# The down projection of a hybrid decoder block: eight products of halves, or seven with weight sums made in DRAM

## The chip, the cores and the metric

The kernel runs on one core of one Trainium2 chip. The metric is device time in microseconds (us) of one execution, the median of three runs. A profile comes from one further execution, taken by the hardware profiler; its own time stands in the table below.

## The reference

One decoder layer on 512 tokens of 1024 channels, all in float32. Only the second half matters here:

```python
h = rms_norm(x, g_ffn_pre)
up = h @ w_up                                   # 1024 -> 2 x 3072
gate_h = causal_dwconv(up[..., :D_FF], ffn_conv_w, ffn_conv_b)
hid = jax.nn.gelu(gate_h) * up[..., D_FF:]      # 512 x 3072
x = x + rms_norm(hid @ w_down, g_ffn_post)      # the down projection, 3072 -> 1024
ple_gate = jax.nn.sigmoid(rms_norm(x, g_ple_gate) @ w_ple_gate)
ple = rms_norm(p @ w_ple_proj, g_ple_post)
x = x + ple_gate * ple
```

Before it stand an input projection with a pooling mixer and a gated linear recurrence, their output projections and `w_o`; they are the same in both kernels.

## The kernel before

Every float32 product is made of three matmuls of a narrower type: an operand is split into a high part (`hi`, a cast on ScalarE) and a rest (`lo`, a subtraction on VectorE), and `mm3` issues high x high, high x low and low x high. So each weight block that arrives (`raw`, 128 x 1024) costs ScalarE one cast and VectorE one subtraction before TensorE can use it.

The instructions of TensorE stand in the order of the code. Those of the other engines are put in order by a scheduler that goes by priority, and each engine then runs its own queue strictly in order: an instruction that waits holds up all that stand behind it. `urgent()` raises a priority. Loads are issued from SP's queue; POOL (GpSimd) does nothing but the small power operation of `rsqrt`, twenty times on one column after once on four.

Weights follow one list, `order`, filled by `plan(key, ap)`. `weight(key, ahead)` prepares up to four blocks past the one that is used. `raw`, `hi` and `lo` have six buffers each, so a block's cast can run once TensorE is done with the block six places earlier.

The up projection (`up_product`) already uses seven products in place of eight for each pair of hidden blocks: tokens and channels are halved, sums of weight blocks are formed on VectorE (`add`), and products named 1 to 7 are accumulated and copied between banks. `gated_half` makes the gate (two shifted multiply-adds on VectorE, a gelu on ScalarE) and `hidden` multiplies it into `hid[j]`, for j from 0 to 23.

The down projection before is `token_major("wd", 12, hid_split)`. 24 weight blocks of 256 x 512 are each used by two k-blocks, four token tiles of 128 and `mm3`: 24 x 2 x 4 x 3 = 576 matmuls of 512 columns. Eight banks hold the eight outputs (token tile `t`, half `h`). The last three block pairs run token tile by token tile, so the tiles finish one after another; after each, `add_norm` adds the normed result to the residual `x3`, `x3n` is scaled for the gate, and `x3_tile(t)` transposes it (two times four PE transposes, L710) and splits it for the last product with `w_ple_gate` ("wpg"). Tiles 2 and 3 are transposed after the first two tiles of that last product.

In the names of the rows below, `A` and `C` are large buffers (four of each), `m` are small ones, `ps` are PSUM banks, `t` are temporaries, and `wsum` are the four new tensors in DRAM.

Of the kernel before, what the change touches and what calls it, by code (L numbers as in the profile page):

```python
# [8 lines left out]
F32 = mybir.dt.float32  # L9
# [4 lines left out]
P = 128  # L14
# [21 lines left out]
PLE_AT = 3  # L36

# [30 lines left out]
def block_kernel(  # L68
# [26 lines left out]
    mid = ctx.enter_context(tc.tile_pool(name="mid", bufs=26))  # L95
    tmp = ctx.enter_context(tc.tile_pool(name="tmp", bufs=5))
    small = ctx.enter_context(tc.tile_pool(name="small", bufs=16))
    psum = ctx.enter_context(tc.tile_pool(name="psum", bufs=8, space=bass.MemoryType.PSUM))
# [102 lines left out]

    def seven(p):

        return [(p - (f == 3), f) for f in (SEVEN if p > 1 else SEVEN_1) if (f == 3 or p < NPAIR) and (f != 3 or p > 1)]
# [31 lines left out]
    for kp in range(12):  # L236
        for h in range(2):
            plan(("wd", kp, h), rows2(w_down, kp, h))
# [88 lines left out]


    def rsqrt(v, n=1):
        y = tiny(n)  # L330
        nc.gpsimd.tensor_tensor(y, v, mhalf[:, :n], ALU.pow)  # L331
        return y
# [50 lines left out]
    rstd1 = rsqrt(v4, NT)  # L383
    diag = temp()
# [454 lines left out]
    def hidden(j, pu, q):  # L839
        hid[j] = slot()  # L840
        if q is not None:
            V.tensor_tensor(
                hid[j].rearrange("p (b c) -> p b c", b=2),
                pu.rearrange("p (b c) -> p b c", b=2),
                q[:, None, :].to_broadcast([P, 2, HALF]),
                ALU.add,
            )
            pu = hid[j]
        V.tensor_tensor(hid[j], act_g[j], pu, ALU.mult)
# [33 lines left out]
    for i in range(2):  # L883
        hidden(i, ub[i], None)
# [5 lines left out]

    for p in range(1, NPAIR + 1):
# [11 lines left out]
    g_fpost = gains(G_FFN_POST)  # L903
    ple = [quad("C", F32), quad("C", F32)]
    for a in range(2):
        nc.sync.dma_start(
            ple[a].rearrange("p (a h) c -> p a (h c)", a=2),
            pled[2 * a * P : 2 * (a + 1) * P, :].rearrange("(a p) c -> p a c", p=P),
        )


    x3 = []
    for a in range(2):
        xt = quad("C", F32)
        nc.sync.dma_start(
            xt.rearrange("p (a h) c -> p a (h c)", a=2),
            x2d[2 * a * P : 2 * (a + 1) * P, :].rearrange("(a p) c -> p a c", p=P),
        )
        x3.append(xt)
    g_pg = gains(G_PLE_GATE)  # L920
    hs = {}

    def hid_split(k, t):
        g = k // 4
        if g not in hs:
            hs[g] = quad("A"), quad("A")
            for q in range(4):
                split(hs[g][0][:, q, :], hs[g][1][:, q, :], hid[4 * g + q])
        return tuple(s[:, k % 4, t * P : (t + 1) * P] for s in hs[g])
# [3 lines left out]

    def x3_tile(t):
        for h in range(2):
            ps = transposed(x3n[t, h])
            x3t[t, h] = slot(F32R), slot(F32R)
            with urgent():
                split(*x3t[t, h], ps)

    for t, i, pair in token_major("wd", 12, hid_split):
        if i == 3 and t >= 2:
            x3_tile(t - 2)
        if i != 5:
            continue
        res = [x3[t // 2][:, 2 * (t % 2) + h, :] for h in range(2)]
        with urgent():
            add_norm(pair, g_fpost, res)
            for h in range(2):
                n = slot()  # L950
                V.tensor_tensor(n, res[h], g_pg[h], ALU.mult)
                x3n[t, h] = n
        s3 = rstd_of(res)
        r3[t] = const.tile([P, 1], F32, tag=f"r3{t}", name=f"r3{t}")
        V.tensor_copy(r3[t], s3)
# [97 lines left out]
```

## Time and profile before

| | us |
|---|---|
| median of three runs (lowest, highest) | 765.53 (765.23, 765.67) |
| the profiled execution, its own time | 765.22 |
| its span from first to last instruction | 763.4 |
| TensorE busy in the span | 758.2 (99%) |
| VectorE, ScalarE, POOL busy | 524.0, 406.3, 15.2 |
| mean share of the DMA engines on the one busy queue | 35.9% |
| first matmul of the down projection | 581.21 |
| first matmul of the product with `w_ple_gate` | 713.58 |

Matmuls overlap each other in the records (one of 512 columns is shown as 0.39 us long), so their cost is read from start to start, not from the durations. Stretches of time are given as from:to in us of the span.

### The profile page before, as it was taken

The page shows a single profiled execution, that of the slowest core. Times are in us where ns is not written, and L with a number is a line of the kernel's source. Part 1 is how long each engine was busy: PE and PEld are TensorE (multiplying, and loading weights), DVE is VectorE, ACT ScalarE, POOL GpSimd, SP SyncE. Part 2 cuts the span into 40 slices and gives each one's busy share as a digit, 9 for nine tenths or more (in the row PEclk, how much of TensorE's full clock was granted, in tenths as well). Part 3 has the DMA queues.
Part 4 walks back from the last instruction along what each step waited for, and adds up shares of the span by engine and source line. Part 5 has one row for each costly group of instructions (what it writes and reads, how often), then busy time and mean ns, then how long its engine had stood idle before and what let it go on. Part 6 is the DMA issues. An engine that isn't in the chain of part 4 may idle for free.

```text
span 763.4 us, 11051 instructions
## 1 busy us (share of the span) xinstructions
PE 758.2 (99%) x4377; PEld 669.6 (88%) x4377; DVE 524.0 (69%) x709; ACT 406.3 (53%) x642; POOL 15.2 (2%) x27
## 2 busy tenths in 40 slices
PE   9999999999999999999999999999999999999997
PEld 8887788888888888899999999999999888888886
DVE  4897537998345573589998888888988332335852
ACT  6746779835233251377766666666675322224631
POOL 0000000000000000010000000000000000001100
PEclk9999999999999999999999999999999999999999
DMA  8842222133223449222243233333369332320111
GB/s 333 308 164 82 84 70 84 35 137 124 91 97 124 165 142 327 83 93 80 79 150 104 95 95 111 111 112 111 111 222 316 125 103 91 108 86 0 56 56 55
DMA packets 42163, 93.87 MB, mean 123 GB/s; under 512 B 3456, under 2 KB 4096, under 8 KB 42112
## 3 DMA queue, kind: packets, MB, share of 16 engines
q1 hardware_dynamic: 41968, 93.08, 35.9%
q8 instruction: 34, 0.56, 0.3%
q14 instruction: 17, 0.14, 0.1%
q10 hardware_dynamic: 144, 0.10, 0.0%
HBM read 86.87 MB, written 6.29 MB: 122 GB/s over the span
## 4 chain that ended last, share of the span: by engine, by line
PE 96%; DMA 2%; DVE 0%; ACT 0%; SPq 0%; POOL 0%; issue 0%; DVEq 0%
PE ps L173 31%; PE ps L174 31%; PE ps L175 31%; DMA C<-in_x_dram 1%; PE ps L710 1%; PE ps L500 1%; PE ps L395 1%; DMA m<-in_x_t_dram 1%; ACT C L380 0%; SPq L303 0%; DVE lo L164 0%; POOL s L331 0%; PE ps L442 0%; DVE t L386 0%; ACT t L139 0%
## 5 line engine op out<-in xcount | busy, mean ns | idle before, releaser
L164 DVE TENSOR_TENSOR lo<-raw,hi 128x1024 fp32r<-128x1024 f32 (+2 forms) x167 | 193.4, 1179 | 97.9 <-ACT hi L313 71.9
L173 PE MATMUL ps<-A,hi 128*128 128x256 f32 (+1 forms) x608 | 199.8, 329 | 0.0
L174 PE MATMUL ps<-A,hi 128*128 128x256 f32 (+1 forms) x608 | 199.3, 328 | 0.0
L175 PE MATMUL ps<-A,lo 128*128 128x256 f32 (+1 forms) x608 | 199.3, 328 | 0.0
L313 ACT CAST hi<-raw 128x1024 fp32r<-128x1024 f32 (+1 forms) x94 | 94.0, 1008 | 146.0 <-PE ps L174 61.7
L173 PEld LDWEIGHTS ps<-A,hi 128*128 128x128 f32 x608 | 114.5, 188 | 11.3 <-issue 1.1
L175 PEld LDWEIGHTS ps<-A,lo 128*128 128x128 f32 x608 | 114.5, 188 | 10.1
L174 PEld LDWEIGHTS ps<-A,hi 128*128 128x128 f32 x608 | 114.5, 188 | 9.7
L173 PE MATMUL ps<-C,hi 128*128 128x256 f32 (+1 forms) x392 | 117.9, 301 | 0.0
L174 PE MATMUL ps<-C,hi 128*128 128x256 f32 (+1 forms) x392 | 117.8, 301 | 0.0
L175 PE MATMUL ps<-C,lo 128*128 128x256 f32 (+1 forms) x392 | 117.8, 300 | 0.0
L173 PE MATMUL ps<-hi,A 128*128 128x512 f32 x256 | 99.9, 390 | 0.0
L175 PE MATMUL ps<-hi,A 128*128 128x512 f32 x256 | 99.6, 389 | 0.0
L174 PE MATMUL ps<-lo,A 128*128 128x512 f32 x256 | 99.6, 389 | 0.0
L168 ACT CAST hi<-raw 128x1024 fp32r<-128x1024 f32 x70 | 72.5, 1052 | 35.1 <-PE ps L174 24.6
L174 PEld LDWEIGHTS ps<-C,hi 128*128 128x128 f32 x392 | 74.2, 189 | 2.7
L175 PEld LDWEIGHTS ps<-C,lo 128*128 128x128 f32 x392 | 74.2, 189 | 2.5
L173 PEld LDWEIGHTS ps<-C,hi 128*128 128x128 f32 x392 | 74.1, 189 | 2.5
L175 PEld LDWEIGHTS ps<-hi,A 128*128 128x128 f32 x256 | 48.1, 188 | 10.0
L173 PEld LDWEIGHTS ps<-hi,A 128*128 128x128 f32 x256 | 48.1, 188 | 9.8
L174 PEld LDWEIGHTS ps<-lo,A 128*128 128x128 f32 x256 | 48.1, 188 | 9.8
L164 DVE TENSOR_TENSOR A<-m,A 128x512 fp32r<-128x512 f32 x40 | 26.1, 687 | 14.6 <-ACT A L168 14.2
(144 smaller groups left out, 907.3 us busy)
## 6 DMA issues: line engine op xcount, KB each, us to landing
raw<-in_w_up_dram SPq DMA_DIRECT2D x48, 512.0 KB, 3.4
raw<-in_w_in_dram SPq DMA_DIRECT2D x32, 512.0 KB, 3.9
raw<-in_w_down_dram SPq DMA_DIRECT2D x24, 512.0 KB, 3.4
raw<-in_w_rg_out_dram SPq DMA_DIRECT2D x8, 512.0 KB, 3.2
raw<-in_w_o_dram SPq DMA_DIRECT2D x8, 512.0 KB, 3.3
raw<-in_w_ple_gate_dram SPq DMA_DIRECT2D x8, 512.0 KB, 3.3
m<-in_rows_dram SPq DMA_DIRECT2D x10, 256.0 KB, 5.4
m<-in_x_t_dram SPq DMA_DIRECT2D x8, 256.0 KB, 7.1
```

What stands on the lines that cost most here:

```text
L164: V.tensor_tensor(o, a, b, ALU.subtract)
L168: last_copy[0] = ACT.copy(hi, src)
L173: PE.matmul(o, ah, bh, start=start, stop=False, **kw)
L174: PE.matmul(o, ah, bl, start=False, stop=False, **kw)
L175: PE.matmul(o, al, bh, start=False, stop=stop, **kw)
L313: ACT.copy(hi, raw)
L395: PE.matmul(rx[m], a[:, o : o + P], b, start=k == 0 and i == 0, stop=k == KD - 1 and i == 2)
L500: PE.matmul(ps, bd[pr, a, o], b[pr], start=i == 0, stop=i == 2)
L710: PE.transpose(ps[:, q * P : (q + 1) * P], a[:, q * P : (q + 1) * P], ident)
```

## The change

`hid` is cut into halves of tokens (the first and the last 256) and of hidden blocks (even and odd j), `w_down` into halves of hidden blocks and of output columns. Seven products of such halves take the place of eight. They run one after another, in the order 1, 2, 5, 6, 3, 7, 4; each uses six weight blocks of two k-blocks, two token tiles and `mm3`: 6 x 2 x 2 x 3 = 72 matmuls of 512 columns, 504 in all.

The weight sums for products 5, 6, 7 and 4 are not formed on VectorE. `sum_down` has POOL issue 48 transfers of 512 KB from DRAM to DRAM, right behind the first power operation; 24 of them add to what lies there (`accum_op`). The weight list then has 42 blocks for the down projection in place of 24: 18 from `w_down` itself, 24 from the sums.

Differences of `hid` are formed on VectorE (`down_form`): 5 and 6 and 3 step by step in `chain`, 7 in place. Each of 21 forms (three per product) is split into an `A` buffer of 128 x 1024 for each of high and low. The results are put together in banks: `c11` from products 1 and 2, `c12` from `q5`, the bank `zd` and product 3, and so on.

```diff
+DOWN = (1, 2, 5, 6, 3, 7, 4)
+DOWN_TAIL = 3
+NQ = NJ // 4
...
+    wdv = w_down.rearrange("(q a s p) c -> q s p a c", a=2, s=2, p=P)
+    wsum = {f: dram.tile([NQ, P, 2, S], F32, name=f"wsum{f}") for f in (5, 6, 7, 4)}
...
+        def dma(f, q, ap, **kw):
+            ins = nc.gpsimd.dma_start(wsum[f][q], ap, **kw)
+            behind(ins, last[0])
+            last[0] = ins.ins.name
+
+        for q in range(NQ):
+            dma(5, q, down_block(1, q))
+            dma(7, q, down_block(0, q))
+        for q in range(NQ):
+            dma(5, q, down_block(0, q), accum_op=ALU.add)
+            dma(7, q, down_block(3, q), accum_op=ALU.add)
+        for q in range(NQ):
+            dma(6, q, wsum[5][q])
+        for q in range(NQ):
+            dma(6, q, down_block(3, q), accum_op=ALU.add)
+        for q in range(NQ):
+            dma(4, q, wsum[6][q])
+        for q in range(NQ):
+            dma(4, q, down_block(2, q), accum_op=ALU.add)
...
-    for kp in range(12):
-        for h in range(2):
-            plan(("wd", kp, h), rows2(w_down, kp, h))
+    for f in DOWN:
+        for q in range(NQ):
+            plan(("wd", f, q), wsum[f][q] if f in wsum else down_block(f, q))
...
     rstd1 = rsqrt(v4, NT)
+    sum_down(last_pow[0])
...
-    for i in range(2):
-        hidden(i, ub[i], None)
     form_split(5, True)
...
+    mid_pool.__exit__(None, None, None)
+    hpool = ctx.enter_context(tc.tile_pool(name="hid", bufs=6, reuse_waits="tile"))
...
+    for i in range(2):
+        hidden(i, ub[i], None)
...
+        if f == 5:
+            V.tensor_tensor(v, h21, h22, ALU.subtract)
+        elif f == 6:
+            V.tensor_tensor(v, v, h11, ALU.subtract)
+        elif f == 3:
+            V.tensor_tensor(v, v, h12, ALU.add)
+        elif f == 7:
+            V.tensor_tensor(v, h11, h21, ALU.subtract)
+        w = big.tile([P, 2, 4, HALF], F32R, tag="A", name=nm("A"))
+        split(w[:, 0], w[:, 1], v)
...
+    gq = quad("C", F32)
+    for n, i in enumerate((G_FFN_POST, G_PLE_GATE)):
+        nc.sync.dma_start(
+            gq[:, 2 * n : 2 * n + 2, :].rearrange("p h c -> p (h c)"), rows[i : i + 1, :].broadcast_to([P, D])
+        )
...
+    for _ in down_product(1, zd, True):
+        pass
+    for i in range(2):
+        with urgent():
+            ACT.copy(c11[i], zd[i])
+    for _ in down_product(2, c11, False):
+        pass
+    for _ in down_product(5, dd, True):
+        pass
...
+    for _ in down_product(6, zd, False, tail=2):
+        pass
+    for i in range(2):
+        with urgent():
+            V.tensor_tensor(c12[i], q5[:, i], zd[i], ALU.subtract)
...
+    for _ in down_product(3, c12, False, head=2):
+        pass
...
+    for _ in down_product(7, zd, False, tail=2):
+        pass
+    for i in range(2):
+        with urgent():
+            V.tensor_tensor(q5[:, i], q5[:, i], zd[i], ALU.subtract)
...
+    for q in down_product(4, zd, False, head=2, tail=DOWN_TAIL):
+        if q == 1:
+            x3_norm(0, (c11[0], c12[0]))
+        if q == 2:
+            x3_norm(1, (c11[1], c12[1]))
...
+        if q >= NQ:
+            x3_norm(q - NQ + 2, (zd[q - NQ], q5[:, q - NQ]))
+        if 1 < q < NQ + 1:
+            x3_tile(0 if q < NQ else 1)
```

Within a product, `head` and `tail` say how many weight blocks at its start and end run token tile by token tile; the blocks between alternate between the two tiles. Tiles 0 and 1 are complete with product 3, tiles 2 and 3 with product 4, which ends with three blocks for tile 2 and then three for tile 3.

Three places of the queues matter for what follows. In the rows, output<-inputs stand by name with a number for each buffer, and the brackets name whose semaphores an instruction waits for. First SP, where the up projection ends. Before, the two loads of `pled` stand ahead of the fifth weight block of the down projection (`raw_5820`):

```order
L305 DMA raw_5768<-in_w_down_dram 128x2x512 [waits DMAHW2_49,DVE_49]
L906 DMA C_5808<-pled 128x2x1024 [waits DMAHW3_49,PE_49]
L906 DMA C_5809<-pled 128x2x1024 [waits DMAHW4_49,PE_49]
L305 DMA raw_5820<-in_w_down_dram 128x2x512 [waits DMAHW5_49,DVE_49]
L305 DMA raw_5864<-in_w_down_dram 128x2x512 [waits DMAHW6_49,DVE_49]
```

With the change, two broadcasts of the norm gains stand there, into the third of the `C` buffers, ahead of the fifth block (`raw_5848`):

```order
L344 DMA raw_5808<-in_w_down_dram 128x2x512 [waits DMAHW2_49,DVE_49]
L1062 DMA C_5845<-in_rows_dram 128x1024 [waits DMAHW3_49,PE_49]
L1062 DMA C_5845<-in_rows_dram 128x1024 [waits DMAHW4_49]
L344 DMA raw_5848<-in_w_down_dram 128x2x512 [waits DMAHW5_49,DVE_49,Activation_49]
L344 DMA raw_5872<-in_w_down_dram 128x2x512 [waits DMAHW6_49,DVE_49,Activation_49]
```

The third `C` buffer before the down projection holds part of the activations that the last pair's product 4 reads, so the queue waits there for that product, where it waited before for the pair's product 1.

At the same place on VectorE, before, with the last pair's gate (`t_5758`, `t_5763`) and hidden blocks (`m_5798`, `m_5801`):

```order
L833 SCALAR_TENSOR_TENSOR t_5758<-ps_5541,col,t_5758 128x511 [waits Activation_49]
L833 SCALAR_TENSOR_TENSOR t_5758<-ps_5541,col,t_5758 128x510 [waits DVE_49]
L833 SCALAR_TENSOR_TENSOR t_5763<-ps_5555,col,t_5763 128x511 [waits Activation_49]
L842 TENSOR_TENSOR m_5798<-ps_2977,t_5726 128x512 [waits PE_49]
L833 SCALAR_TENSOR_TENSOR t_5763<-ps_5555,col,t_5763 128x510 [waits DVE_49]
L849 TENSOR_TENSOR m_5798<-t_5758,m_5798 128x512 [waits DVE_49,Activation_49]
L842 TENSOR_TENSOR m_5801<-ps_2990,t_5726 128x512 [waits PE_49]
L164 TENSOR_TENSOR lo_5823<-raw_5820,hi_5822 128x1024 [waits DMAHW5_49]
L849 TENSOR_TENSOR m_5801<-t_5763,m_5801 128x512 [waits DVE_49,Activation_49]
```

And with the change, up to the split of the third form of product 1 (`A_5908`), which takes in those hidden blocks (`h_5167`):

```order
L875 SCALAR_TENSOR_TENSOR t_5798<-ps_5583,col,t_5798 128x511 [waits Activation_49]
L170 TENSOR_TENSOR lo_5851<-raw_5848,hi_5850 128x1024 [waits DMAHW5_49,PE_49,Activation_49]
L875 SCALAR_TENSOR_TENSOR t_5798<-ps_5583,col,t_5798 128x510 [waits DVE_49]
L875 SCALAR_TENSOR_TENSOR t_5803<-ps_5597,col,t_5803 128x511 [waits Activation_49]
L884 TENSOR_TENSOR h_5167<-ps_3029,t_5766 128x512 [waits PE_49]
L875 SCALAR_TENSOR_TENSOR t_5803<-ps_5597,col,t_5803 128x510 [waits DVE_49]
L891 TENSOR_TENSOR h_5167<-t_5798,h_5167 128x512 [waits DVE_49,Activation_49]
L884 TENSOR_TENSOR h_5170<-ps_3042,t_5766 128x512 [waits PE_49]
L170 TENSOR_TENSOR lo_5875<-raw_5872,hi_5874 128x1024 [waits DMAHW6_49]
L891 TENSOR_TENSOR h_5170<-t_5803,h_5170 128x512 [waits DVE_49,Activation_49]
L170 TENSOR_TENSOR lo_5893<-raw_5890,hi_5892 128x1024 [waits DMAHW7_49,Activation_49]
L170 TENSOR_TENSOR A_5908<-h_5167,A_5908 128x1024 [waits Activation_49]
```

The split of the fifth weight block, which stood behind the first hidden block, now stands ahead of most of the gate's work.

The third place is VectorE where the product with `w_ple_gate` begins. Before, the fourth of its weight blocks (`lo_6559`) stands right behind the first two operations of tile 3's norm:

```order
L164 TENSOR_TENSOR m_6716<-ps_6710,m_6715 128x512 [waits Activation_49]
L164 TENSOR_TENSOR m_6725<-ps_6719,m_6724 128x512 [waits Activation_49]
L702 TENSOR_TENSOR t_6740<-ps_5848,m_5804 128x512 [waits PE_49]
L702 TENSOR_TENSOR t_6742<-ps_5882,m_5805 128x512 [waits PE_49]
L164 TENSOR_TENSOR lo_6559<-raw_6556,hi_6558 128x1024 [waits DMAHW2_49]
```

With the change, that block (`lo_6809`) stands behind the whole norm of tile 2, the split of tile 1 (`h_6773`) and the start of tile 3's norm:

```order
L744 TENSOR_TENSOR t_6743<-ps_2941,C_5845 128x512 [waits PE_49]
L744 TENSOR_TENSOR t_6745<-sum_6208,C_5845 128x512
L382 SCALAR_TENSOR_TENSOR s_6753<-s_6747,s_6750 128x1 [waits Activation_49]
L747 SCALAR_TENSOR_TENSOR C_6577<-t_6743,s_6755,C_6577 128x512 [waits Pool_49]
L747 SCALAR_TENSOR_TENSOR C_6577<-t_6745,s_6755,C_6577 128x512 [waits DVE_49]
L1047 TENSOR_TENSOR h_6699<-C_6577,C_5845 128x512 [waits DVE_49] x2
L170 TENSOR_TENSOR h_6773<-ps_6774,h_6773 128x512 [waits PE_49,Activation_49]
L170 TENSOR_TENSOR h_6773<-ps_6781,h_6773 128x512 [waits PE_49,Activation_49]
L744 TENSOR_TENSOR t_6818<-ps_2942,C_5845 128x512 [waits PE_49]
L744 TENSOR_TENSOR t_6820<-sum_6208,C_5845 128x512
L382 SCALAR_TENSOR_TENSOR s_6767<-s_6761,s_6764 128x1 [waits Activation_49]
L170 TENSOR_TENSOR lo_6809<-raw_6806,hi_6808 128x1024 [waits DMAHW0_49]
```

The norm of tile 2 has moved closer to the end of the down projection, from one tile's 36 matmuls ahead of tile 3 to 18.

On POOL, all 48 transfers stand between the first power operation (`s_185`) and the second one, of the embedding's norm.

More of the change, by code (lines that the diff above doesn't have):

```diff
@@ L326, in pick @@
         return t[0][:, a:b], t[1][:, a:b]
+    last_pow = [None]
     def rsqrt(v, n=1):
         y = tiny(n)
-        nc.gpsimd.tensor_tensor(y, v, mhalf[:, :n], ALU.pow)
+        last_pow[0] = nc.gpsimd.tensor_tensor(y, v, mhalf[:, :n], ALU.pow).ins.name
         return y
@@ L839, in hidden @@
     def hidden(j, pu, q):
-        hid[j] = slot()
+        hid[j] = hslot(j)
         if q is not None:
@@ L889, in block_kernel, with hquad, hslot @@
     form_split(3, True)
+    mid_pool.__exit__(None, None, None)
+    hpool = ctx.enter_context(tc.tile_pool(name="hid", bufs=6, reuse_waits="tile"))
+    def hquad(dt=F32):
+        return hpool.tile([P, 4, S], dt, tag="h", name=nm("h"))
+    hq = {}
+    def hslot(j):
+        k = j % 2, j // 8
+        if k not in hq:
+            hq[k] = hquad()
+        return hq[k][:, j // 2 % 4, :]
+    for i in range(2):
+        hidden(i, ub[i], None)
     for p in range(1, NPAIR + 1):
@@ L901, in block_kernel @@
                     hidden(2 * q + i, ub[i], q5[q][:, i * HALF : (i + 1) * HALF])
-    g_fpost = gains(G_FFN_POST)
-    ple = [quad("C", F32), quad("C", F32)]
-    for a in range(2):
-        nc.sync.dma_start(
[L907 to L916, printed above, removed]
+    zd = [zb[0], zb[1]]
@@ new lines, in block_kernel, with quarter, link, down_form @@
+    c11, c12 = [gb[0], gb[1]], [ub[0], ub[1]]
+    dd = [db, bank()]
+    chain = [quad("C", F32), quad("C", F32)]
+    def quarter(b, k, m):
+        return hq[k, m][:, :, b * HALF : (b + 1) * HALF]
+    def link(m):
+        return chain[m // 2].rearrange("p (m a) (b c) -> p m (a b) c", m=2, b=2)[:, m % 2]
+    down = {}
+    def down_form(f, m):
+        if (f, m) in down:
+            return
+        h11, h12, h21, h22 = (quarter(b, k, m) for b in range(2) for k in range(2))
+        v = {1: h11, 2: h12, 4: h22, 7: h21}.get(f) if f in (1, 2, 4, 7) else link(m)
+        if f == 5:
[8 more added lines that the diff above has]
+        split(w[:, 0], w[:, 1], v)
+        down[f, m] = w
@@ new lines, in ahead_form, with down_product, piece @@
+    def ahead_form(f, m):
+        n = 3 * DOWN.index(f) + m
+        if n < 3 * len(DOWN):
+            down_form(DOWN[n // 3], n % 3)
+    def down_product(f, banks, start, head=0, tail=0):
+        def piece(q, i, last):
+            w = weight(("wd", f, q), ahead=AHEAD if last else 1)
+            down_form(f, q // 2)
+            for a in range(2):
+                k = 2 * q + a
+                v = down[f, k // 4][:, :, k % 4, i * P : (i + 1) * P]
+                mm3(
+                    banks[i],
+                    (v[:, 0], v[:, 1]),
+                    pick(w, a * S, (a + 1) * S),
+                    start and k == 0,
+                    k == 2 * NQ - 1,
+                    skip_group_check=True,
+                )
+        cuts = sorted({0, head, *range(head, NQ - tail), NQ - tail, NQ})
+        for q, e in zip(cuts, cuts[1:]):
+            for i in range(2):
+                for n in range(q, e):
+                    piece(n, i, i == 1 or n == q)
+                    if i == 1 and n % 2 == 0:
+                        ahead_form(f, n // 2 + 1)
+                if e - q == tail and e == NQ:
+                    yield NQ + i
+            if e < NQ or not tail:
+                yield e - 1
@@ L917, in block_kernel, with load_x3 @@
+    x3 = [None, None]
+    def load_x3(a):
+        x3[a] = quad("C", F32)
+        nc.sync.dma_start(
+            x3[a].rearrange("p (a h) c -> p a (h c)", a=2),
             x2d[2 * a * P : 2 * (a + 1) * P, :].rearrange("(a p) c -> p a c", p=P),
         )
[L919 to L929, printed above, removed]
@@ L931, in block_kernel, with x3_norm @@
     x3t, r3 = {}, {}
     x3n = {}
[L934 to L945, printed above, removed]
+    def x3_norm(t, pair):
         res = [x3[t // 2][:, 2 * (t % 2) + h, :] for h in range(2)]
-        with urgent():
-            add_norm(pair, g_fpost, res)
+        with tc.high_priority(offset=URGENT if t > 1 else 0):
+            add_norm(pair, (gq[:, 0, :], gq[:, 1, :]), res)
```

37 lines of the change are left out of this document (33 added, 4 removed).

## The prediction

> **What bounds the kernel now.** I read the page's busy times first, then the clock, then the chain of work that ended last.
>
> ```profile
> span 763.4 us, 11051 instructions
> PE 758.2 (99%) x4377; PEld 669.6 (88%) x4377; DVE 524.0 (69%) x709; ACT 406.3 (53%) x642; POOL 15.2 (2%) x27
> PEclk9999999999999999999999999999999999999999
> PE 96%; DMA 2%; DVE 0%; ACT 0%; SPq 0%; POOL 0%; issue 0%; DVEq 0%
> ```
>
> TensorE is busy from end to end at full clock, and the chain is 96% its own work. A matmul taken away shortens the time as long as no other engine becomes late; a wait put before a matmul lengthens it in full. So I need the pace of the matmuls, and what VectorE and the transfers have left in the stage that changes. For the pace I read TensorE's rows in time order: the first matmul of the down projection, two rows 116 matmuls apart (118 rows from one end to the other, the first being 597.55), the transposes, and the first matmul of the next product.
>
> ```profile
> 581.21 0.40 PE L173 MATMUL ps<-hi,A 128*128 128x512 f32 x1
> ...
> 597.55 0.39 PE L173 MATMUL ps<-hi,A 128*128 128x512 f32 x1
> ...
> 624.07 0.39 PE L173 MATMUL ps<-hi,A 128*128 128x512 f32 x1
> ...
> 700.91 1.03 PE L710 MATMUL ps<-ident,m 128*128 128x128 f32 x8
> 701.70 0.48 PE L173 MATMUL ps<-hi,A 128*128 128x512 f32 x1
> ...
> 713.58 0.39 PE L173 MATMUL ps<-hi,m 128*128 128x512 f32 x1
> ```
>
> From 581.21 to 713.58 are 132.37 us; two tiles' transposes take 0.79 each (700.91 to 701.70), so 576 matmuls took 130.8: 0.227 each. From 597.55 to 624.07 are 26.52, and 26.52 / 117 is 0.227 too. One product of 72 will take 16.35.
>
> Next VectorE and ScalarE: the same stage, and one pair of the up projection ahead of it, in the view by stretches (busy time and count of PE, PEld, DVE, ACT, POOL; clock; DMA share; GB/s); then groups by line.
>
> ```profile
> 581.40:713.80 132.40, 132.40 (x593) 109.77 (x592) 56.97 (x76) 44.15 (x71) 2.71 (x5) 1.00 0.32 106
> 420.00:439.00 19.00, 19.00 (x160) 19.00 (x160) 16.54 (x19) 12.35 (x20) 0.00 (x0) 1.00 0.29 95
> L164 DVE TENSOR_TENSOR lo<-raw,hi 128x1024 fp32r<-128x1024 f32 x23 | 28.0, 1224 | 47.3 <-ACT hi L313 47.3
> L313 ACT CAST hi<-raw 128x1024 fp32r<-128x1024 f32 x24 | 25.1, 1051 | 53.0 <-PE ps L175 50.5 <-issue 2.6
> L257 DVE TENSOR_TENSOR raw<-raw,raw 128x1024 f32<-128x1024 f32 x22 | 26.8, 1219 | 3.3 <-DMA raw<-in_w_up_dram 3.3
> L821 ACT COPY t<-ps 128x512 f32<-128x512 f32 x11 | 6.4, 581 | 1.9 <-PE ps L175 1.9
> L164 DVE TENSOR_TENSOR A<-m,A 128x512 fp32r<-128x512 f32 x40 | 26.1, 687 | 14.6 <-ACT A L168 14.2 <-PE ps L175 0.3
> ```
>
> VectorE is 43% busy in the down projection (57.0 of 132.4) and waits for casts, which wait for TensorE to free a buffer. There is room, but the change will fill it.
>
> **The change part by part.**
>
> *Matmuls.* 576 become 504. 72 x 0.227 = 16.35 us saved, on the path. The transposes stay, eight for each tile.
>
> *VectorE in the products.* Each product has six weight splits and three form splits of 128 x 1024 (1.22 each), and products 5, 6, 3 and 7 three differences of that size (1.22 too): 9 or 12 operations, 11.0 or 14.7 us of 16.35. Besides come four bank differences and four norms. It fits in every product, at up to 90%. A weight block can be split six blocks ahead and a form four forms ahead of its use, so lateness within a product is covered by some 10 us of lead. Hidden: 0. If the spacing of these operations were above 16.35 / 12 = 1.36 us, the cover would go and the stage would run at VectorE's pace.
>
> *ScalarE.* 9 casts of 1.05 = 9.5 of 16.35 per product, plus copies. The copy of product 1 into the bank of product 2 (0.58) has six matmuls, 1.36 us, since the two token tiles alternate. 0; if the copy came a cast late, about 0.5.
>
> *Where the up projection ends.* The early forms and differences (6 x 1.22 = 7.3 us, less the eight early splits of before, 8 x 0.687 = 5.5) lie in VectorE's spare 2.5 us per pair and the 4.9 us that no next pair's sums need: 0. But the fifth weight block is loaded later. Here are the page's row for these loads (KB, median us to landing), SP's queue, transfers of the stretch 555:600, and the gate's operations:
>
> ```profile
> raw<-in_w_down_dram SPq DMA_DIRECT2D x24, 512.0 KB, 3.4
> ...
> 578.40 0.37 SPq L915 DMA_DIRECT2D C<-x2d  x1
> 578.82 0.93 SPq L625 DMA_DIRECT2D m<-in_rows_dram  x2
> ...
> raw<-in_w_down_dram SPq DMA_DIRECT2D x12, 512.0 KB, 6.2
> ...
> m<-in_rows_dram SPq DMA_DIRECT2D x4, 256.0 KB, 9.1
> L833 DVE SCALAR_TENSOR_TENSOR t<-ps,col,t 128x510 f32<-128x510 f32 x24 | 17.8, 742 | 0.1
> L842 DVE TENSOR_TENSOR m<-ps,t 128x512 f32<-128x512 f32 x22 | 14.3, 682 | 0.5 <-PE ps L175 0.5
> L849 DVE TENSOR_TENSOR m<-t,m 128x512 f32<-128x512 f32 x22 | 14.9, 686 | 0.4
> ```
>
> At 578.40 the queue's wait for the pair's product 4 ended, with a load into that third C buffer. In the change the two gain broadcasts go out there, 0.47 apart, and the fifth block at about 579.3. It lands between 582.7 (3.4 later, the page's median for such a load alone) and 588.4 (9.1 later). I take 584.8: 5.5 after its issue, near the 6.2, since less is in flight than at that place before. Behind the landing stand, in order: its cast 1.05, its split 1.22, three gate steps of 0.74, an addition 0.68, a product 0.69, an addition 0.68, a split 1.22, a product 0.69, a split 1.22, and the form's split 1.22 (the gelus lie beside). That is 10.9, less 0.08 of overlap at each of ten joins (a split below starts at 715.44, lasts 1.21, and the next begins at 716.57): 10.1. The form is ready at 594.9. TensorE needs it at the third matmul of the fifth block: 581.21 + 4 x 12 x 0.227 + 2 x 0.227 = 592.55. A wait of 2.4, bounds 0.3 and 6.0.
>
> *Where the next product begins.* The norm chain of a tile, from the second bank's arrival to the scaled result, in VectorE's rows, and the fourth block's split after it:
>
> ```profile
> 704.72 0.69 DVE L702 TENSOR_TENSOR t<-ps,m 128x512 f32<-128x512 f32 x1 [0.67 <-PE ps L175]
> 706.23 0.16 DVE L341 SCALAR_TENSOR_TENSOR s<-s,s 128x1 f32<-128x1 f32 x1 [0.81 <-ACT t L338]
> 707.11 1.42 DVE L705 SCALAR_TENSOR_TENSOR C<-t,s,C 128x512 f32<-128x512 f32 x2 [0.72 <-POOL s L331]
> 708.44 1.29 DVE L951 TENSOR_TENSOR m<-C,m 128x512 f32<-128x512 f32 x2
> ...
> 715.44 1.21 DVE L164 TENSOR_TENSOR lo<-raw,hi 128x1024 fp32r<-128x1024 f32 x1
> 716.57 0.15 DVE L341 SCALAR_TENSOR_TENSOR s<-s,s 128x1 f32<-128x1 f32 x1
> ```
>
> 704.72 to 709.73 is 5.0. In the change both first operations stand after tile 2's bank is done: 5.6 to 6.1, take 6.0. Then two splits of 0.69, two operations of tile 3, and the fourth block's split: 6.0 + 1.4 + 1.4 + 0.15 + 1.2 = 10.1, less overlaps 9.9. Tile 2 ends 18 x 0.227 + 0.87 of transposes = 4.95 before the down projection's end E; the split is done at E + 5.0. It is needed at the second matmul of the fourth block, E + 19 x 0.227 = E + 4.3. A wait of 0.7, bounds 0 and 2; before, it was done 3.07 after 713.58, with 1.2 to spare.
>
> *The 48 transfers.* They compete for the DMA engines, and they occupy POOL's queue ahead of later power operations:
>
> ```profile
> 20.15 1.03 POOL L331 TENSOR_TENSOR s<-s,mhalf 128x4 f32<-128x4 f32 x1 [18.84 <-DVE s L382]
> 249.45 0.54 POOL L331 TENSOR_TENSOR s<-s,mhalf 128x1 f32<-128x1 f32 x1 [228.27 <-DVE s L341]
> ...
> raw<-in_w_bd_dram SPq DMA_DIRECT2D x1, 512.0 KB, 11.4
> ...
> 20.00:25.00 5.00, 4.86 (x21) 3.68 (x20) 3.85 (x10) 4.70 (x8) 1.03 (x1) 1.00 1.03 402
> 30.00:35.00 5.00, 5.00 (x23) 4.13 (x22) 5.00 (x11) 4.98 (x7) 0.00 (x0) 1.00 0.74 252
> ```
>
> No row shows a transfer from DRAM to DRAM or one that adds. Bounds for one of 512 KB: 1.3 us (at the 402 GB/s of a full queue) and 11.4 (a load in that full queue). I take 3.4, the lone load: 48 x 3.4 = 163, so they end near 185, while POOL's next power operation comes at 249.45. Hidden: 0. Early on they share full DMA engines until about 30 us, where loads in flight may double; blocks come several products ahead of use there, so 0 to 4, taken as 0.
>
> The Trainium skill speaks against free transfers: "DMA: Bandwidth & Descriptors" (Anatomy of one DMA — SWDGE (gpsimd) path) fits 2.0 us plus bytes over 436 GB/s per DMA from this queue, and "Collectives: The Full Stack" (The bandwidth ceiling) says that an adding transfer reads two sources and runs at half the rate. By these, as an estimate, 24 x 3.2 + 24 x 4.4 = 182 us in a row, an end near 204, and the same sum. No run here shows it yet.
>
> *Other edits.* The moved `hidden` calls of the first pair and 18 more loads on SP (0.37 each, 16.35 / 6 = 2.7 apart) lie beside TensorE: 0.
>
> *Sum.* 765.22 - 16.35 + 2.4 + 0.7 = 751.97 against the profiled execution, which lies 0.31 under the median 765.53. Against the median: 752.3.
>
> **The rivals.**
> - *VectorE becomes the bound.* For it: 90% in four of seven products, many waits for casts. Against: in the up projection it works at 16.5 of 19 without holding TensorE. If each operation needs 1.5 us with its waits, four products take 18.0 and one or two more lose a little: +7 to +12, 759 to 764.
> - *The early loads suffer.* For it: the 1.03 share at 20 to 25. Against: the blocks' lead. +2 to +6: 754 to 758.
> - *POOL's queue is late (slower).* The embedding's norm waits for POOL behind the transfers, VectorE waits for that norm in order, and TensorE runs dry some 10 us later. It decides from (249.45 - 21.2) / 48 = 4.75 us per transfer. At 6 us: 21 + 288 = 309, 60 late, less 10: about 802. For it: unknown adding rate, and eight in flight at most. Against: a lone load of 3.4.
> - *The gain is eaten at the joins.* Both joins at their worst and more of the kind: around 765.
>
> **How the numbers follow.** Forecast 0.60, its own range 749.2 (no waits) to 757 (6.0 + 2 at the joins). VectorE bound 0.13, early loads 0.13, POOL late 0.09, eaten 0.05. The predicted time is the likeliest's, 752.3. The range 749 to 760 leaves out POOL late, eaten and half of VectorE bound, 0.2. Less than 0.2% (1.5 us) can't be told from no change here. Faster: 0.60 + 0.13 + 0.12 = 0.85; same: 0.05; slower: 0.10.
>
> **What would show it.** Right: matmuls of a product spaced 0.227, the stage some 117 us long, one gap of 1 to 5 us at the fifth block's third matmul, one under 2 us at the fourth block of the next product, POOL's last transfer issued well before 249. Wrong: VectorE rows without idle time in products 5 to 7 and TensorE waiting for `lo` again and again; power operations that start late; gaps before 62 us.

## The result, and the profile after

| | median | runs | profiled execution | its span |
|---|---|---|---|---|
| before | 765.42 us | 765.23 to 765.67 (4) | 765.22 | 763.4 |
| changed | 751.68 us | 751.51 to 751.71 (4) | 751.66 | 749.9 |

The ratio is 0.982, 95% interval 0.9803 to 0.9837: 13.7 us less. Two executions in this document, 811.15 of the run with 72 more copies and 829.66 of the kernel before beside it, ran at a granted clock of 0.851 and stand in no range below. The prediction said 752.3, between 749 and 760. The total is right. Two of its three terms are not, and 2 us of the time come from something that it did not look at.

The page of the changed kernel, lines that answer to those shown of before:

```profile
span 749.9 us, 11094 instructions
PE 744.7 (99%) x4305; PEld 656.5 (88%) x4305; DVE 569.3 (76%) x740; ACT 434.9 (58%) x661; POOL 57.0 (8%) x75
PEclk9999999999999999999999999999999999999999
PE 99%; DVE 0%; ACT 0%; issue 0%
```

72 matmuls are gone, VectorE has 45 us more to do, and TensorE is still the whole chain. So the question is how long TensorE needs for each stretch. Its rows at the borders, first of the changed kernel (first matmul of the down projection, first of the next product, last of all), then the last one of before:

```profile
582.53 0.40 PE L179 MATMUL ps<-hi,A 128*128 128x512 f32 x1
...
698.85 0.40 PE L179 MATMUL ps<-hi,h 128*128 128x512 f32 x1
...
745.44 0.28 PE L181 MATMUL ps<-hi,h 128*128 128x256 f32 x1
```

```profile
759.09 0.28 PE L175 MATMUL ps<-hi,m 128*128 128x256 f32 x1
```

| stretch | before, us | changed, us | difference | predicted |
|---|---|---|---|---|
| up to the down projection | 581.21 | 582.53 | +1.32 | 0 |
| down projection | 132.37 | 116.32 | -16.05 | -16.35 + 2.4 |
| next product, to its last matmul | 45.51 | 46.59 | +1.08 | +0.7 |
| after it, to the end of the span | 4.3 | 4.5 | +0.15 | 0 |
| sum | 763.4 | 749.9 | -13.5 | -13.25 |

The down projection has no wait of 1 to 5 us anywhere. The largest irregularities of TensorE behind 582 are these two, 0.14 and 0.10 us over the normal step:

```profile
680.24 0.39 PE L181 MATMUL ps<-hi,A 128*128 128x512 f32 x1
680.61 0.47 PE L179 MATMUL ps<-hi,A 128*128 128x512 f32 x1
...
703.29 0.50 PE L180 MATMUL ps<-lo,h 128*128 128x512 f32 x1
703.62 0.40 PE L181 MATMUL ps<-hi,h 128*128 128x512 f32 x1
```

And the 1.32 us ahead of the down projection are not a wait either. At 64 us the changed kernel is 0.15 us behind, at 166 it is 0.11; between 166 and 286 it falls back by another 1.2 us without one gap. Here are two places where the same matmuls run in both, each as a first row and the row 12 matmuls later; before:

```profile
278.21 0.39 PE L173 MATMUL ps<-hi,m 128*128 128x512 f32 x1
...
280.93 0.39 PE L173 MATMUL ps<-m,hi 128*128 128x512 f32 x1
...
728.75 0.39 PE L175 MATMUL ps<-hi,m 128*128 128x512 f32 x1
...
731.48 0.39 PE L175 MATMUL ps<-hi,m 128*128 128x512 f32 x1
```

changed:

```profile
279.39 0.40 PE L179 MATMUL ps<-hi,m 128*128 128x512 f32 x1
...
282.19 0.40 PE L179 MATMUL ps<-m,hi 128*128 128x512 f32 x1
...
728.48 0.39 PE L181 MATMUL ps<-hi,h 128*128 128x512 f32 x1
...
731.28 0.39 PE L181 MATMUL ps<-hi,h 128*128 128x512 f32 x1
```

Before, 12 matmuls take 2.72 us, 0.2267 each; in the changed kernel 2.80, 0.2333 each, with the clock granted in full and no other engine named. (An operand list reads moving, stationary: `hi,m` streams a weight past a stationary tile of `mid`.) Only matmuls with an operand in `mid` or `hid`, and those in between them, are longer. From all rows, joined with the addresses of the built program: between 166 and 290, 108 matmuls with a moving operand in `mid` take 0.2307 on average, 48 with a stationary one 0.2332, the 386 others there 0.2278; together 1.2 us over 0.2267.

What the diff did to these tiles is one line: `mid` is opened behind `tmp` and `small`, so that its place can be given to `hid` later. It moved in SBUF by 11072 bytes.

### The profile page after: what moved, and what is told of

Its sections match the earlier page's. It is cut to its first block, busy times and chain, and to the rows that moved or that the text cites. A ratio compares the mean times of both kernels' runs of the same rounds, so it can differ in the third digit from the quotient of the medians.

```text
span 749.9 us, 11094 instructions
## 1 busy us (share of the span) xinstructions
PE 744.7 (99%) x4305; PEld 656.5 (88%) x4305; DVE 569.3 (76%) x740; ACT 434.9 (58%) x661; POOL 57.0 (8%) x75
## 4 chain that ended last, share of the span: by engine, by line
PE 99%; DVE 0%; ACT 0%; issue 0%
PE ps L179 31%; PE ps L180 31%; PE ps L181 31%; PE ps L437 3%; PE ps L752 1%; PE ps L542 1%; PE ps L197 1%; PE ps L484 0%; ACT t L145 0%; DVE t L1126 0%; DVE t L1127 0%; PE ps L853 0%; DVE ones L189 0%; DVE mhalf L191 0%
## 5 line engine op out<-in xcount | busy, mean ns | idle before, releaser
L170 DVE TENSOR_TENSOR lo<-raw,hi 128x1024 fp32r<-128x1024 f32 (+2 forms) x185 | 215.4, 1183 | 61.5 <-ACT hi L352 42.1
L352 ACT CAST hi<-raw 128x1024 fp32r<-128x1024 f32 (+1 forms) x112 | 113.4, 1016 | 132.5 <-PE ps L180 67.1
L179 PE MATMUL ps<-hi,A 128*128 128x512 f32 x232 | 90.7, 391 | 0.0
L181 PE MATMUL ps<-hi,A 128*128 128x512 f32 x232 | 90.3, 389 | 0.0
L180 PE MATMUL ps<-lo,A 128*128 128x512 f32 x232 | 90.3, 389 | 0.0
L372 POOL TENSOR_TENSOR s<-s,mhalf 128x1 f32<-128x1 f32 (+1 forms) x21 | 17.3, 822 | 577.4 <-DVE s L382 558.6
L179 PEld LDWEIGHTS ps<-hi,A 128*128 128x128 f32 x232 | 43.6, 188 | 9.3 <-ACT hi L352 0.4
L181 PEld LDWEIGHTS ps<-hi,A 128*128 128x128 f32 x232 | 43.5, 188 | 9.1
L180 PEld LDWEIGHTS ps<-lo,A 128*128 128x128 f32 x232 | 43.6, 188 | 8.8
## 6 DMA issues: line engine op xcount, KB each, us to landing
raw<-in_w_in_dram SPq DMA_DIRECT2D x32, 512.0 KB, 10.3
```

What stands on the lines that cost most here:

```text
L170: V.tensor_tensor(o, a, b, ALU.subtract)
L179: PE.matmul(o, ah, bh, start=start, stop=False, **kw)
L180: PE.matmul(o, ah, bl, start=False, stop=False, **kw)
L181: PE.matmul(o, al, bh, start=False, stop=stop, **kw)
L352: ACT.copy(hi, raw)
L372: last_pow[0] = nc.gpsimd.tensor_tensor(y, v, mhalf[:, :n], ALU.pow).ins.name
```

## The experiments

Twelve kernels ran. Times are medians; the kernel before, run beside them, stayed between 765.3 and 765.44. One of the twelve leaves part of the computation out; its expectation says which.

### Where the tiles lie

Four kernels that differ in addresses alone (the order of the instructions on every engine is the same). In the changed kernel:

```diff
-    small = ctx.enter_context(tc.tile_pool(name="small", bufs=16))
+    small = ctx.enter_context(tc.tile_pool(name="small", bufs=18))
```

> In the changed kernel TensorE never idles long, yet it reaches the down projection 1.32 us later than before, and its last products run at 0.2333 per matmul of 512 columns in place of 0.2267. Both hold for matmuls with an operand in the mid or hid tiles, which the change moved in SBUF so that they begin at a multiple of 128 bytes; all other tiles begin 64 past one. This kernel is the changed one with two more small buffers, which put mid and hid 64 bytes further; nothing else moves. Theory (start addresses): all matmuls of 512 columns run at 0.2267, the drift between 166 and 286 is gone, and the time falls by 2.0 to 2.5 us to about 749.4. Rivals (a lower clock late in the run, or the 48 transfers' traffic, or the tiles' place high in SBUF): no change, 751.7.

```diff
-    warm = const.tile([P, 1], F32, tag="warm", name="warm")
+    warm = const.tile([P, 17], F32, tag="warm", name="warm")
```

> The changed kernel with one small constant 64 bytes longer, ahead of all the other pools: weights, forms and big tiles now begin at a multiple of 128 bytes, mid and hid 64 past one. If what costs is a difference between the two operands' start addresses modulo 128, the same matmuls are slow, about 751.7. If a start at a multiple of 128 is slow for whichever operand has it, nearly all 2000 matmuls of 512 columns get 4 to 7 ns longer: 757 to 764. If mid and hid alone matter, 749.4.

Both edits together:

> Both shifts: all matmul operands begin at a multiple of 128 bytes. If a difference between the operands costs: 749.4 as with the first shift, matmuls of 512 columns at 0.2267. If a start at a multiple of 128 is slow by itself: 757 to 764. Those of 256 columns with a stationary operand at such a start ran at 0.1178 in the changed kernel, against 0.1200 otherwise; if that comes from the stationary operand's start alone, 2036 of them save 2.2 ns each, another 4.5 us: about 745.

And in the kernel before, `small` with 18 buffers opened ahead of `mid`:

> The kernel before with its small buffers placed ahead of mid and two more of them, so that the mid tiles begin at a multiple of 128 bytes while the other tiles begin 64 past one. Theory (start addresses): the last products run at 0.2333, the same drift appears between 166 and 286, and the kernel is slower by 2.0 to 2.5 us: about 767.7. Rivals (transfers, clock late in the run, or the place high in SBUF): no change, 765.4.

Measured: 751.47, 751.48, 751.64, and 767.52 for the kernel before (ratio 1.0027, 1.0017 to 1.0037). So moving `mid` by 576 bytes (`tmp` moves with it) does cost the old kernel 2.2 us, which needs neither the transfers nor anything else of the change; but the start modulo 128, the theory of these four runs, is not what matters, since equal starts won nothing. What the runs have in common is the distance between `mid` and the other operands (weights, forms and big tiles all lie multiples of 512 bytes from each other), taken modulo 512:

| kernel | first weight buffer | first `mid` tile | distance mod 512 | 512 columns, stationary in `mid` or `hid`, end of the kernel |
|---|---|---|---|---|
| before | 20800 | 164160 | 0 | 0.2268 |
| changed | 20800 | 175232 | 320 | 0.2333 |
| small +2 | 20800 | 175296 | 384 | 0.2324 |
| warm longer | 20864 | 175296 | 320 | 0.2333 |
| both | 20864 | 175360 | 384 | 0.2323 |
| before, `small` ahead | 20800 | 164736 | 64 | 0.2334 |

The test of that was made with 22 small buffers, which bring the distance back to a multiple of 512:

```diff
-    small = ctx.enter_context(tc.tile_pool(name="small", bufs=16))
+    small = ctx.enter_context(tc.tile_pool(name="small", bufs=22))
```

> The first theory fell in half: a shift of mid in the kernel before cost 2.2 us, as said, but equal starts modulo 128 in the changed kernel won nothing. In the runs so far the matmuls with a mid or hid operand are at 0.2267 where mid and the other tiles lie a multiple of 512 bytes apart (before: 143360 = 280 x 512), and at 0.231 to 0.2333 where they lie 320 (changed), 384 (both shifted runs) or 64 (before, shifted) past one. This kernel is the changed one with six more small buffers: 192 bytes, so that the distance becomes 154624 = 302 x 512. Theory (distance modulo 512, the size of one stationary tile's row): all matmuls of 512 columns at 0.2267, 2.0 to 2.4 us less than the changed kernel, about 749.3. Rival (the place of mid high in SBUF, or a multiple of 2048, the size of a whole row): no change, 751.6.

Measured: 749.72 (749.54 to 750.29), 1.96 less than the changed kernel; ratio to before 0.9795 (0.9781 to 0.9808). TensorE's rows at the borders and at the place shown above:

```profile
581.18 0.40 PE L179 MATMUL ps<-hi,A 128*128 128x512 f32 x1
...
697.50 0.39 PE L179 MATMUL ps<-hi,h 128*128 128x512 f32 x1
...
728.39 0.39 PE L180 MATMUL ps<-lo,h 128*128 128x512 f32 x1
...
731.11 0.39 PE L180 MATMUL ps<-lo,h 128*128 128x512 f32 x1
...
743.31 0.28 PE L181 MATMUL ps<-hi,h 128*128 128x256 f32 x1
```

The down projection begins at 581.18 as before (581.21), 12 matmuls take 2.72 again, and the last product needs 45.81 in place of 46.59. The distance theory holds, and its rivals, a place of `mid` high in SBUF and a period of 2048 bytes, are out (154624 is not a multiple of 2048). The down projection itself is 116.32 long in both.

The same quantity, used on purpose. First 64 bytes between the weights' pool and the big tiles:

```diff
+    gap = ctx.enter_context(tc.tile_pool(name="gap", bufs=1))
+    gap.tile([P, 16], F32, tag="gap", name="gap")
     big = ctx.enter_context(tc.tile_pool(name="big", bufs=4))
```

> The changed kernel with 64 unused bytes between the weights' pool and the big tiles (forms and their like), so that these two lie 64 past a multiple of 512 apart. Matmuls of 256 columns took 0.1200 each in the up projection, and 0.1134 to 0.1178 in the last tile where the stationary operand lay in a shifted pool. Theory A (what slows 512 columns speeds 256): 2000 matmuls of the up projection save 6.6 ns, 13 us, and some 1100 of 512 columns between forms and weights lose 4 to 6.6, 4 to 7 us: 743 to 747. Theory B (only 512 columns care): 755 to 759. Rival (addresses don't matter): 751.6.

Measured: 753.13. Neither theory: matmuls of 256 columns in the up projection went from 0.1200 to 0.1178, those of 512 columns to 0.229 where the moving operand had been moved and to 0.2333 where the stationary one had (the whole down projection). 2036 x 2.2 ns are 4.5 us won; 504 + 187 at 6.6 ns and some 800 behind 62 us at 2.2 ns are 6.3 lost, the difference 1.8 against 1.45 measured. The direction of the distance matters, and matmuls of 256 and 512 columns answer to it in opposite ways. So only tiles that serve as moving operands of 256 columns should be moved, and so that the stationary one lies 64 bytes past a multiple of 512 from them and not 64 short of it; the C tiles come nearest to that:

```diff
     big = ctx.enter_context(tc.tile_pool(name="big", bufs=4))
+    gap = ctx.enter_context(tc.tile_pool(name="gap", bufs=1))
+    gap.tile([P, 112], F32, tag="gap", name="gap")
+    bigc = ctx.enter_context(tc.tile_pool(name="bigc", bufs=4))
...
-    small = ctx.enter_context(tc.tile_pool(name="small", bufs=16))
+    small = ctx.enter_context(tc.tile_pool(name="small", bufs=24))
...
-        return big.tile([P, 4, S], dt, tag=tag, name=nm(tag))
+        return (bigc if tag == "C" else big).tile([P, 4, S], dt, tag=tag, name=nm(tag))
```

> Distance modulo 512 as a free choice: mid a multiple of 512 from the weights as in the faster run (749.7), and the C tiles alone 448 past one (64 below the weights' place). They are the moving operand of some 980 matmuls of 256 columns in the up projection and of 190 of 512 columns. A distance of 64 the same way round gave 0.1134 to 0.1136 for 256 columns in the last tile (0.1200 at no distance) and 0.2333 for 512. Theory (the distance sets both): 980 x 6.6 ns less, 190 x 6.6 ns more, 5.2 us less: about 744.5. Middle (0.1178, as with the big tiles 64 above): 2.2 us less from 256 columns, 0.4 to 1.3 more: 748 to 749. Rival (only the last tile is like that): 750 to 751.

Measured: 745.88 (745.47 to 746.14), ratio to before 0.9744 (0.9731 to 0.9757): 5.8 us less than the changed kernel, 3.8 less than the one with 22 small buffers, and the fastest of all. A stretch of the up projection in the changed kernel, a row and the one 12 matmuls later, and the same in this one:

```profile
497.09 0.28 PE L181 MATMUL ps<-C,lo 128*128 128x256 f32 x1
...
498.53 0.28 PE L181 MATMUL ps<-C,lo 128*128 128x256 f32 x1
```

```profile
497.07 0.28 PE L183 MATMUL ps<-C,hi 128*128 128x256 f32 x1
...
498.43 0.28 PE L183 MATMUL ps<-C,hi 128*128 128x256 f32 x1
```

1.44 us against 1.36: 0.1200 and 0.1133 each. Over the whole up projection those with a moving C tile took 0.1149 (979), those with an A tile 0.1196; the 189 of 512 columns with a moving C tile went to 0.2333, as foreseen. The 3.8 us are less than the 5.2 expected because not all C tiles reached 0.1133: the first 216 matmuls of 256 columns, and 24 behind one of 512 at 377.51, ran at 0.1178 (1.41 us for 12), and those that follow matmuls with an A tile at 0.1133 after the first few. Tiles and distance are the same in both cases:

```profile
377.74 0.28 PE L182 MATMUL ps<-C,hi 128*128 128x256 f32 x1
...
379.15 0.28 PE L182 MATMUL ps<-C,hi 128*128 128x256 f32 x1
```

### What the transfers cost

> The changed kernel without the 48 transfers; products 5, 6, 7 and 4 load plain blocks of the weight in place of the sums, so the sums are left out. Theory (transfers hidden, as in the prediction): 0 to 0.3 us less, since TensorE was only 0.13 us later at 64 us than before: 751.4 to 751.7. Rival (they slow loads or TensorE all the way to 136 us or beyond): 1 us or more less, and the drift between 166 and 286 is gone.

The call of `sum_down` is left out and `down_block(f % 4, q)` is loaded for every product. Measured: 751.62, no difference to 751.68. TensorE begins the down projection at 582.24, 0.29 earlier than the changed kernel, which is within what the profiled executions differ by at 64 us (the one with 18 small buffers is 0.84 behind the kernel before there):

```profile
582.24 0.40 PE L179 MATMUL ps<-hi,A 128*128 128x512 f32 x1
```

The drift between 166 and 286 stays. The transfers are hidden to within some 0.3 us. To see what a late POOL costs:

```diff
+        for f in 3 * (5, 6, 7, 4):
+            for q in range(NQ):
+                dma(f, q, down_block(1, q))
         for q in range(NQ):
             dma(5, q, down_block(1, q))
```

> The changed kernel with 72 more plain copies into the sums' places ahead of the 48 transfers (they are overwritten afterwards). At the 2.4 us per transfer of the changed kernel 120 transfers end at 21 + 288 = 309, the very case of the prediction's third rival, 60 us past POOL's next power operation. Theory (that rival): TensorE runs dry some 10 us after it, and the kernel takes some 40 to 50 us longer: 792 to 802. Rival (what waits for POOL has more lead, or plain copies go faster): less, and the gap starts later than 260.

Measured: 763.81 in the profiled execution (762.12 to 764.04 in four), 12.1 more than the changed kernel and far under the theory's 792 to 802. That is the run's rival: less, and a gap that starts behind 260. POOL's rows and then TensorE's around the wait (in brackets the idle time and what ended it):

```profile
274.36 1.05 POOL L375 TENSOR_TENSOR s<-s,mhalf 128x1 f32<-128x1 f32 x1
```

```profile
268.62 0.39 PE L181 MATMUL ps<-C,lo 128*128 128x512 f32 x1
276.25 0.79 PE L179 MATMUL ps<-hi,m 128*128 128x512 f32 x1 [7.24 <-DVE m L687]
276.84 0.63 PE L180 MATMUL ps<-lo,m 128*128 128x512 f32 x1
277.27 0.63 PE L181 MATMUL ps<-hi,m 128*128 128x512 f32 x1
```

120 transfers took (274.4 - 21.1) / 120 = 2.1 us each, so the power operation came at 274.36 and not at 250.31. TensorE ran dry some 19 us after that operation had been due, waited 7.2 us for VectorE, ran seven matmuls at 0.43, and waited another 2.1 us at 334, behind which its pace was the normal one. The rival's mechanism is real and its "less 10" is about right (24 late, 12 lost). What was wrong is how near it is: at the changed kernel's own pace POOL is free 114 us early.

### The fifth block

```diff
     gq = quad("C", F32)
+    V.tensor_copy(gq[:, 0, :1], weight(("wd", 1, 3), ahead=0)[1][:, :1])
```

> The prediction's wait of 2.4 us at the fifth block did not come: the gain broadcasts went out at 562.4 and not at 578.4, since they took the first of the four C buffers to come free, not the third, and the fifth block's load went out at 568.8. Here a copy of one column from the fourth block's low part into the gains' tile, ahead of their loads, holds them until that split is done, near 579.3, the time that the prediction assumed. If its chain of terms was right (landing, cast, split, gate steps, form), TensorE waits 2.4 us (0.3 to 6.0) near 593.9 and the time is 752 to 758, likeliest 754.0. Rival (VectorE's order adapts and hides the late landing): 751.6.

Measured: 751.95, and nothing tested. The scheduler let the second gain load go at 562.4, six weight loads behind it, and only the first waited until 579.56. The next kernel holds both (the copy writes to the place of both, and the fifth block's load is set behind them in SP's queue):

> The run before let one gain load go at 562.4 and the other six weight loads ahead of the held one, so the fifth block wasn't late and nothing was tested. Here both gain loads wait for the fourth block's split (done near 579.2) and the fifth block's load stands behind them, as the prediction had it. By its chain of terms TensorE waits 2.4 us (0.3 to 6.0) near 594: 752.0 to 757.6, likeliest 754. Rival (VectorE's order now does the gate and the form ahead of that split, so the chain behind the landing is one cast and one split, 2.2 us): lands at 585 to 589, ready by 591.5, no wait, 751.7 to 752.0.

Measured: 751.79, no wait. SP's queue, and VectorE's rows at the place:

```profile
579.78 0.82 SPq L1066 DMA_DIRECT2D C<-in_rows_dram  x2
580.69 10.19 SPq L345 DMA_DIRECT2D raw<-in_w_down_dram  x8
```

```profile
586.93 1.21 DVE L170 TENSOR_TENSOR A<-h,A 128x1024 fp32r<-128x1024 f32 x1
588.06 2.43 DVE L170 TENSOR_TENSOR lo<-raw,hi 128x1024 fp32r<-128x1024 f32 x2
```

The loads stand at the times that the prediction assumed, but the gate's operations and the form's split now run ahead of the fifth block's split (588.06) and not behind it, and that split is done by 589.3, before TensorE asks for it near 594. Since the edit let the scheduler place VectorE's work anew, a late landing in the order as it was built was not tried.

### VectorE

```diff
         split(w[:, 0], w[:, 1], v)
+        for _ in range(2):
+            sub(w[:, 1], v, w[:, 0].bitcast(F32))
         down[f, m] = w
```

> The changed kernel with each of the 21 forms' low part computed three times in place of once: 6 more operations of 128 x 1024 per product. Their pace in the changed kernel was 1.136 us where nothing waited. Theory (VectorE at 9 or 12 operations has room, at 15 or 18 it is the bound): four products of 18 need 20.4 us in place of 16.35, three of 15 need 17.0, together 18 us more, less up to 10 of lead: 760 to 770, TensorE waits for low parts in products 5 to 7. Rival (more lead than thought): 752 to 756.

Measured: 786.68, 35.0 more (the profiled execution 788.70): VectorE is the bound, and the cost is nearly double what was expected. The first row is VectorE's room in the changed kernel, from the view by stretches over its down projection (PE, PEld, DVE, ACT, POOL busy; clock; DMA share; GB/s):

```profile
582.53:698.85 116.32, 116.32 (x523) 96.13 (x522) 97.23 (x104) 72.42 (x91) 4.61 (x5) 1.00 0.67 217
```

Of the kernel with the added subtractions, a row of the waits (total, times, longest) and TensorE's rows behind one of them:

```profile
PEld ps L181 <- DVE A L170: 19.3, 10, 5.0
```

```profile
632.02 0.39 PE L180 MATMUL ps<-lo,A 128*128 128x512 f32 x1
636.00 0.80 PE L181 MATMUL ps<-hi,A 128*128 128x512 f32 x1 [3.59 <-DVE A L170]
636.59 0.63 PE L179 MATMUL ps<-hi,A 128*128 128x512 f32 x1
```

The view by stretches over its down projection, and over a part behind that wait:

```profile
582.75:736.20 153.45, 131.07 (x523) 103.97 (x522) 145.42 (x149) 75.28 (x95) 4.85 (x5) 0.91 0.49 165
636.60:641.50 4.90, 4.90 (x13) 3.84 (x12) 4.90 (x5) 0.79 (x1) 0.00 (x0) 0.50 0.29 107
```

42 more operations at 1.137 are 47.8 us; VectorE had 116.3 - 97.2 = 19.1 us to spare; 28.7 are too much. The stage grew by 37.1, from 116.32 to 153.44, so VectorE used 11 of its 19 idle us; it is busy 145.42 us, 95%, and about half of the 8.0 left is idle time behind 702, at the last joins and norms. Behind each longer wait TensorE runs at 0.43 per matmul in place of 0.227 for some microseconds, at a granted clock of 0.50: 43 matmuls, 8.7 us. Whether these add to the stage is not shown; behind the wait at 636.00 VectorE is busy without a break all the while. The Trainium skill, "TensorE: Matmul & The Clock Gate" (HAM oscillation — how this bites in real kernels), warns of idle gaps over about 3.4 us, behind which the clock is halved. The traces agree on the half pace and are stricter on the gap: a wait of 2.2 us was enough here once, while one of 2.1 in the run with more copies and one of 0.85 were not.

## Why the prediction was right, and where it was wrong

That the total came out so close is luck: two waits that did not come (2.4, and 0.4 of 0.7) and a slowdown that was not foreseen (2.0 to 2.1) cancel. The range holds by the largest term, which was right. By its own steps:

- *Matmuls, -16.35.* Right: 504 at 0.2267, the stage 116.32 long (it said some 117), 16.05 shorter. The missing 0.3 is spread, 0.14 of it at 680.24. (The two rows that its pace is read from are 117 matmuls apart, as its division has it, not 116.)
- *The fifth block, +2.4.* Wrong; it was 0. The step that failed is "with a load into that third C buffer": the gain broadcasts were taken to wait until 578.40. The scheduler gave them the first of the C buffers to come free, and the queue was done with them 16 us earlier. Here are SP's queue and the fifth block's split in the changed kernel:

```profile
562.44 0.82 SPq L1062 DMA_DIRECT2D C<-in_rows_dram  x2
568.84 18.59 SPq L344 DMA_DIRECT2D raw<-in_w_down_dram  x8
```

```profile
580.87 1.21 DVE L170 TENSOR_TENSOR lo<-raw,hi 128x1024 fp32r<-128x1024 f32 x1
...
588.64 1.22 DVE L170 TENSOR_TENSOR A<-h,A 128x1024 fp32r<-128x1024 f32 x1
```

  That split is done at 582.1, 11.8 us before its use. The chain's last term, the form's split at 588.64, is done at 589.9, 4.0 us before the matmul at 593.88 that needs it. From the first to the end of the last are 9.0 us, and the prediction's terms behind the cast give 9.1: these were sized right; the block's load ahead of them went out at 568.84 and not at 579.3. The order of the built program names tiles without saying which buffer each one gets; the number of allocations in the code does not tell it either, and the chain of ten terms rested on that guess.
- *The next product's fourth block, +0.7.* Right in place, too large: the block's split (`lo`) was done 4.4 us after the end of the down projection (703.24 less 698.85) and not 5.0. With the addresses repaired, the last product takes 45.81 against 45.51 before: 0.3.

```profile
702.02 1.22 DVE L170 TENSOR_TENSOR lo<-raw,hi 128x1024 fp32r<-128x1024 f32 x1
```

- *VectorE hidden, 0.* Right: 84% busy over the stage. Its rival's mechanism shows when 19 us are exceeded, as the run above did.
- *The 48 transfers hidden, 0.* Right, and each cheaper than the 3.4 taken: POOL was free at 136.3, (136.3 - 21.1) / 48 = 2.4 each, and the last transfer landed at 151.6, 16.3 us after its issue. POOL's rows in the changed kernel (the bracket is its wait for the transfer eight places earlier, in the last row but one for the copy that it adds to, six places earlier):

```profile
28.56 0.65 POOL L222 DMA_DIRECT2D wsum<-in_w_down_dram  x1 [1.82 <-DMA wsum<-in_w_down_dram]
...
56.56 1.04 POOL L222 DMA_DIRECT2D wsum<-in_w_down_dram  x1 [1.17 <-DMA wsum<-in_w_down_dram]
60.46 1.03 POOL L222 DMA_DIRECT2D wsum<-in_w_down_dram  x1 [2.86 <-DMA wsum<-in_w_down_dram]
...
86.76 0.49 POOL L222 DMA_DIRECT2D wsum<-wsum  x1 [3.12 <-DMA wsum<-in_w_down_dram]
...
135.30 1.03 POOL L222 DMA_DIRECT2D wsum<-in_w_down_dram  x1 [0.63 <-DMA wsum<-wsum]
250.31 0.57 POOL L372 TENSOR_TENSOR s<-s,mhalf 128x1 f32<-128x1 f32 x1 [113.99 <-DVE s L382]
```

  The plain ones, 1 to 12, made way for the next at 28.56 to 56.56: 2.5 us each. The adding ones, 13 to 21, did so at 60.46 to 86.76: 3.3 each, with copies in flight beside them from 73.92 on. But the last six adding ones, with nothing behind them, landed from 138.9 to 151.6, 2.5 each, so a fixed rate for adding is not in these rows. The page of the Trainium skill that the prediction named, "Collectives: The Full Stack" (The bandwidth ceiling), has half the rate for a collective's step that adds, because it reads two sources; here an adding transfer took between once and one and a third times the 2.5 of a plain one. By the other, "DMA: Bandwidth & Descriptors" (Anatomy of one DMA — SWDGE (gpsimd) path), the prediction estimated 182 us in a row; with up to eight in flight the last landed 130.5 us after the first was issued.
- *Early loads, 0.* Right, 0.15 us at 64 us, though the loads of the input projection went from 3.9 to 10.3 us each:

```profile
raw<-in_w_in_dram SPq DMA_DIRECT2D x32, 512.0 KB, 10.3
```

- *Not in the sum at all:* the place of `mid` and `hid`. Of the two stretches where the changed kernel lost time, +1.32 and +1.08, the repair of the addresses gave back 1.35 (0.14 of it lies ahead of 64 us and is not the addresses') and 0.78. The diff showed that `mid` is opened later; it was read as a change of lifetime, and its address was not considered.

## What to carry to other kernels

A pool that is opened at another place moves tiles, and tiles at another distance can change the pace of every matmul that uses them: compare the spacing of the same matmuls before and after, also far from the edit, before a loss is looked for in waits. When a sum agrees with the measurement, take it apart by stretches anyway; here two errors of 2 us hid each other by luck. And where a predicted wait hangs on which buffer a tile gets, read the addresses of the built program instead of counting allocations.

## What was not expected of the hardware

- The step between matmuls of the narrower type (fp32r) depends on where their operands lie in SBUF. By the address of the stationary operand less that of the moving one, modulo 512 bytes, in us, as measured in these kernels:

| distance | 512 columns | 256 columns |
|---|---|---|
| 0 | 0.2267 | 0.1200 |
| 64 | 0.2333 | 0.1133 or 0.1178 |
| 128 | 0.2322 | |
| 192 | 0.2307 | |
| 320 | 0.2333 | 0.1136 or 0.1178 |
| 384 | 0.2324 | 0.1200 |
| 448 | 0.229 | 0.1178 |

  143360, 154624 and 155136 bytes all behave as 0; whether a period of 256 would do was not tried. With 256 columns the distance is not all of it: at 64 both paces stand in one execution, as shown above, and at 320 kernels with the same addresses differ in the last product (0.1178 in the changed kernel, 0.1136 in the one without transfers). What ran just before seems to count too. Why it is so stays open.
- The Trainium skill, "TensorE: Matmul & The Clock Gate" (Step-by-step: what each phase is for), says that two independent read ports let the next weights load without taking bandwidth from the running matmul. No run here shows the weight load's part by itself; what they show is that with fp32r operands the pace changed by 3% and 5% with the addresses alone.
- A wait of 2.2 us of TensorE was followed by seven matmuls at 0.43 in place of 0.2267, one of 3.6 us by thirteen: 1.4 and 2.6 us of TensorE's time on top of the wait. One of 2.1 us was followed by none, so no threshold can be read from these runs.
